# Two more up chunks of each SwiGLU by seven block products, and residues of 105 weight pieces summed by DMAs

## The chip, the cores and the metric

One core of one Trainium2 chip runs the whole program. The metric is the device time of one execution in microseconds. The kernel before takes 2181.22 us, the median of three runs (2180.66 to 2183.26).

## The reference, cut to what matters

A decoder trunk of two layers on 256 tokens of width 2048, in float32. Layer 0 mixes by two groups of attention heads, layer 1 by latent attention; the change leaves both alone. Each layer ends in a SwiGLU feed-forward network (FFN) of inner width 5632:

```python
def swiglu(x, w_gate, w_up, w_down):
    return (jax.nn.silu(x @ w_gate) * (x @ w_up)) @ w_down

for layer in range(DEPTH):            # DEPTH = 2
    ...                               # y = mixer(x)
    x = layer_norm(DEEPNORM_ALPHA * x + y, ln_g[layer, 0], ln_b[layer, 0])
    y = swiglu(x, ffn_w_gate[layer], ffn_w_up[layer], ffn_w_down[layer])
    x = layer_norm(DEEPNORM_ALPHA * x + y, ln_g[layer, 1], ln_b[layer, 1])
```

## The kernel before

**Splitting.** TensorE (PE) multiplies float32 numbers that are rounded (fp32r). To keep accuracy, each operand is split into a rounded part and a residue, and a product is three matmuls: rounded by rounded, rounded by residue, residue by rounded (`mm3`, lines 115 to 118; PE's moving operand is the weight, the stationary one the tokens). `XH` and `XL` hold the two parts of the FFN's input, `YH` and `YL` those of its inner activations.

**Pieces and visits.** Weights come in *chunks* of 512 columns, and a chunk in *pieces* of 256 rows (512 KB). An FFN has gate chunks g0 to g10 and up chunks u0 to u10 of eight pieces each, and down chunks in five groups of four (d0 to d4, after ups 1, 3, 5, 7 and 10). The list `visits` gives the order in which PE uses the pieces; all else follows it. A *plain* visit is 12 matmuls of 512 columns: two blocks of 128 rows, two blocks of tokens, three passes. Chunks marked `S` (gates 1 to 10) are done as seven block products in place of eight, in the manner of Strassen and Winograd: `emit_s` issues 21 matmuls of 256 columns (lines 426 to 428), with sums of blocks of the weights and sums of blocks of the tokens (the tiles `XS`, which `xs_batch` makes in four batches at the start of each FFN). An `S` chunk has four PSUM banks A, B, C, D. When its eighth visit is issued, `drain_s` (lines 456 to 462) adds them up: ACT copies a part of A, then five DVE sums follow, the last two of which read the tile written before; the gate's Silu on ACT comes right behind (line 1023).

**The interleave.** `ffn_part` first lists the plain visits of an FFN in the order u0, u1, d0, u2, u3, d1 and so on (`flat`), and then puts the `S` visits between them: a counter `want` grows by 0.61 per plain visit for 14 visits, then by 0.527, and when it passes a whole number the next gate piece is put in. An up that ends is multiplied on DVE with its gate (`u_done`, line 1027), and `h_T` turns the product by PE transposes after the next plain visits (`after_up`) and splits it into `YH` and `YL`.

**Feeding.** For each piece, in the order of the list, SyncE (SP) issues a load into a raw buffer (`feed_dma`, line 336; four for plain pieces, two, `sraw`, for `S` pieces, and a few more elsewhere). `feed_split` then takes a free pair of weight buffers (in the FFNs four plain pairs `wh`, `wl` and two `S` pairs `sh`, `sl`), and issues for a plain piece the rounding on ACT (line 400) and the residue on DVE (line 402). For an `S` piece `split_s` issues at once the three block differences on DVE (lines 358 to 361, in place in the raw buffer), and *owes* the rounding on ACT (`hi`, line 364) and the residue on DVE (`lo`, line 367, which also frees the raw buffer). Owed work is paid by `pay`:

```python
            while o["fns"] and (step == "all" or o["age"] >= 1 and step == o["fns"][0][0]):
                o["fns"].pop(0)[1]()
```

Each later split raises the age by one. A plain split pays ahead of raising it, so the second plain split after an `S` piece pays; the split of the next `S` piece raises first and then pays, behind its own differences.

**The order of all this** is the program's: the schedule is manual, each engine runs its instructions in the order of issue, and SP its loads. In the main loop a visit is issued, then the chunk's `done` (the drain and the Silu, or the up's product), then the callbacks, and then the buffers of the visited piece become free and `feed_more` issues splits and loads as long as buffers of the right kind are free. An `S` piece's split so comes behind the visit of the `S` piece two before it.

GpSimd (POOL) has little work: parts of the layer norms and of the attention. It issues no DMA.

Of the kernel before, what the change touches and what calls it, by code (L numbers as in the profile page):

```python
# [9 lines left out]
F32 = mybir.dt.float32  # L10
F32R = mybir.dt.float32r
AF = mybir.ActivationFunctionType
ALU = mybir.AluOpType
# [39 lines left out]
def trunk_kernel(ctx: ExitStack, tc: tile.TileContext, x, ab_w_in, b_f, ab_w_out,  # L53
# [81 lines left out]
    def kmajor(c, hs=None):  # L135
        for h in (range(c.nh) if hs is None else hs):
            visits.append((c, h, (0, 1)))
# [57 lines left out]

    GROUPS = ((0, 1), (2, 3), (4, 5), (6, 7), (8, 9, 10))
    NF = 11
    after_up = {}
    win = {}

    def ffn_part(layer):
        def wide(nm, w, f):
            return add_chunk(f"{nm}{layer}_{f}", "X", K16, ([512], lambda h: rows(
                w[layer], h * 256, [(0, 512, f * 512)])))

        def down(gi):
            grp = GROUPS[gi]
            slots = [4 * (f % 4) + k for f in grp for k in range(4)]
            for n in range(4):
                c = add_chunk(f"d{layer}_{gi}_{n}", "Y", slots, (  # L210
                    [512], lambda h, n=n: rows(
                        w_down[layer], grp[0] * 512 + h * 256, [(0, 512, n * 512)])))
                if gi == len(GROUPS) - 1 and n == 3:
                    (lead_final if layer == 1 else lead_end)(c)
                else:
                    kmajor(c)

        g0 = wide("g", w_gate, 0)
        g0.pair = 0
        lead_begin(g0)  # L220
        base = len(visits)
        for f in range(NF):
            kmajor(wide("u", w_up, f))
            if f in (1, 3, 5, 7):
                down(f // 2)
        down(len(GROUPS) - 1)
        flat = visits[base:]
        del visits[base:]
        ends = {}
        for f in range(NF):  # L230
            e = ends[f] = max(k for k, v in enumerate(flat) if v[0].name == f"u{layer}_{f}")
            after_up[layer, f] = [(v[0].name, v[1], v[2]) for v in flat[e + 1:e + 4]]
        gates = []
        for f in range(1, NF):
            c = wide("g", w_gate, f)
            c.S = True
            gates += [(c, h, (0, 1)) for h in range(8)]
        near = {ends[f] + 2 for f in (1, 3, 5, 7, 9)}
        ns, want = 0, 0.0
        for k, v in enumerate(flat):  # L240
            visits.append(v)
            want = max(want + (0.61 if k < 14 else 0.527), ns + 1 if k in near else 0)
            while ns < min(len(gates), int(want)):
                visits.append(gates[ns])
                ns += 1
                if ns % 8 == 0:
                    assert k < ends[ns // 8] - 1, (k, ns, ends)
        assert ns == len(gates)

    w_out_part("oa", ab_w_out[0])  # L250
    ffn_part(0)
# [89 lines left out]
    owed = []  # L341
# [12 lines left out]
    def split_s(j):  # L354
# [14 lines left out]
        wts[j] = (sh.rearrange("p (q c) -> p q c", c=256), sl.rearrange("p (q c) -> p q c", c=256))  # L369
        return hi, lo  # L370

    def feed_split(j, halves=False, part=None):
        if j >= len(pieces):
            return False
        c, h = pieces[j]
        n = 2 * c.n
        if part != 1:
            got = take(w_free, j) if j in raws else None
            if got is None:
                return False  # L380
            slot_of[j] = got
            if c.S:
                new = split_s(j)
                for o in owed:
                    o["age"] += 1
                pay("act")
                pay("dve")
                owe(j, *new)
                return True
            r = raws.pop(j)  # L390
            wh, wl = got[1]
            wts[j] = (wh[:, :n].rearrange("p (k c) -> p k c", k=2),
                      wl[:, :n].rearrange("p (k c) -> p k c", k=2))
            whole[j] = (r, wh, wl)
        r, wh, wl = whole[j]
        cuts = [(0, c.n), (c.n, n)] if halves or part is not None else [(0, n)]
        if part is not None:
            cuts = [cuts[part]]
        for a, b in cuts:
            nc.scalar.activation(wh[:, a:b], r[:, a:b], AF.Copy)  # L400
            pay("act")
            nc.vector.tensor_tensor(wl[:, a:b], r[:, a:b], wh[:, a:b].bitcast(F32),  # L402
                                    op=ALU.subtract)
            pay("dve")
        if part != 0:
            whole.pop(j)
            raw_free.append(rslot_of.pop(j))
        for o in owed:
            o["age"] += 1
        return True  # L410
# [601 lines left out]
    def ffn_done(layer):  # L1012
        for f in range(NF):
            cg, cu = chunks[f"g{layer}_{f}"], chunks[f"u{layer}_{f}"]

            def g_done(t, cg=cg, f=f):
                gt = ff["gt"][f % 2]
                if not cg.S:
                    nc.scalar.activation(gt[:, t], cg.ps[t][0], AF.Silu)
                elif t == 1:  # L1020
                    drain_s(cg, gt)
                    g_ = gt.rearrange("p t c -> p (t c)")
                    nc.scalar.activation(g_, g_, AF.Silu)

            def u_done(t, cu=cu, f=f):
                h_ = ff["gt"][f % 2][:, t]
                nc.vector.tensor_tensor(h_, h_, cu.ps[t][0], op=ALU.mult)

            def h_T(t, f=f):
                h_ = ff["gt"][f % 2][:, t]  # L1030
                tp = transposes([h_[:, k * P:(k + 1) * P] for k in range(4)])
                y = 4 * (f % 4)
                sl = (slice(None), slice(y, y + 4), slice(t * P, (t + 1) * P))
                hilo(YH[sl], YL[sl], tp.rearrange("p (k c) -> p k c", k=4))

            cg.done, cu.done = g_done, u_done
            for t in (0, 1):
                at(after_up[layer, f][t], lambda h_T=h_T, t=t: h_T(t))
        last = len(GROUPS) - 1
        for gi in range(len(GROUPS)):  # L1040
            for n in range(4):
                c = chunks[f"d{layer}_{gi}_{n}"]
                c.done = lambda t, half=None, c=c, n=n, gi=gi: residual(
                    c.ps[t], t, n, gi == 0, gi == last,
                    fine=(layer == 1 and gi == last and t == 1), half=half)
        at((f"g{layer}_0", 3, (1,)), lambda: (xs_open(), xs_batch(0)))
        for n in (1, 2, 3):
            at((f"g{layer}_0", 4 + n, (0, 1)), lambda n=n: xs_batch(n))
        at((f"g{layer}_0", 7, (0, 1)), lambda: s_window(True))
        at(after_up[layer, NF - 1][2], lambda: s_window(False))  # L1050
        at((f"g{layer}_{NF - 1}", 7, (0, 1)), lambda: xs_close(layer))
# [340 lines left out]
```

## Time and profile before

| | |
|---|---|
| median of three runs | 2181.22 us (2180.66 to 2183.26) |
| the profiled execution | 2182.57 us; span on the core 2180.7 us; mean granted clock 0.994 |
| PE busy | 2141.0 us, 98% of the span |
| DVE, ACT, POOL busy | 1645.9 us (75%), 1058.5 us (49%), 93.0 us (4%) |
| DMA | 410 MB, mean 188 GB/s, 56.6% of 16 engines' time |

The span is the time from the first instruction to the last; the profiled execution's own time lies 1.9 us over it. Busy shares are averages over the whole span, so a stage's limit is read from its own stretch. Matmuls are pipelined: what one costs is the distance from its start to the next one's start, not its printed duration. A number in square brackets behind a timeline row is idle time of the engine ahead of that instruction, with what ended it. "PEclk" is the share of full clock that TensorE was granted, 1.00 or 0.50.

### The profile page before, as it was taken

What the parts mean: (1) busy time and instruction counts of PE and PEld (TensorE: products, weight loads), DVE (VectorE), ACT (ScalarE), POOL (GpSimd) and SP (SyncE); (2) the same over time, 40 slices, a digit from 0 to 9 for tenths busy, and PEclk for the clock granted to TensorE, in tenths of its full rate; (3) what the DMA queues carried; (4) which work ended last, traced back from release to release, by engine and by line L of the source; (5) the groups of instructions that cost most, each with busy time, mean ns of one, the idle gap of its engine ahead of it and who ended that gap; (6) DMA issues with size and microseconds to landing.
All of it is one profiled execution on the core that took longest, in us unless ns stands there. A gap on an engine that the chain in (4) does not pass through costs nothing.

```text
span 2180.7 us, 29603 instructions
## 1 busy us (share of the span) xinstructions
PE 2141.0 (98%) x11562; PEld 1827.3 (84%) x11562; DVE 1645.9 (75%) x2103; ACT 1058.5 (49%) x1240; POOL 93.0 (4%) x142
## 2 busy tenths in 40 slices
PE   9999999989999999999999999999999999999998
PEld 8788888778888888888878898878888888888886
DVE  5555656798878888888756676698888888788875
ACT  4444544354444454444534676344545444444451
POOL 2100000100000000000001331010000000000000
PEclk9999999999999999999999999999999999999999
DMA  8565555445556555565765544725655556555572
GB/s 286 169 201 165 169 178 205 181 164 188 189 193 203 193 193 193 183 202 190 253 196 163 175 130 132 279 97 181 197 197 189 192 193 203 193 177 184 190 277 80
DMA packets 230332, 410.29 MB, mean 188 GB/s; under 512 B 14088, under 2 KB 58160, under 8 KB 229168
## 3 DMA queue, kind: packets, MB, share of 16 engines
q1 hardware_dynamic: 230192, 408.40, 56.6%
q8 instruction: 91, 1.49, 0.3%
q14 instruction: 49, 0.40, 0.1%
HBM read 402.56 MB, written 5.78 MB: 187 GB/s over the span
## 4 chain that ended last, share of the span: by engine, by line
PE 60%; issue 35%; DVE 4%; POOL 1%; ACT 1%; DMA 0%; SPq 0%; DVEq 0%; POOLq 0%; ACTq 0%
PE mm L116 15%; PE mm L117 15%; PE mm L118 15%; PE tp L545 2%; PE att L117 1%; PE att L118 1%; PE att L116 1%; PE sB L427 1%; PE sB L426 1%; PE sA L427 1%; PE sB L428 1%; PE sC L426 1%; PE sC L427 1%; PE sC L428 1%; PE sA L428 1%
## 5 line engine op out<-in xcount | busy, mean ns | idle before, releaser
L400 ACT ACTIVATE wh<-raw 128x1024 fp32r<-128x1024 f32 (+4 forms) x440 | 457.9, 1045 | 573.6 <-PE mm L118 430.3
L402 DVE TENSOR_TENSOR wl<-raw,wh 128x1024 fp32r<-128x1024 f32 (+4 forms) x440 | 531.5, 1212 | 203.2 <-ACT wh L400 194.9
L116 PE MATMUL mm<-wh,XH 128*128 128x512 f32 (+3 forms) x1120 | 442.0, 395 | 0.5 <-ACT wh L400 0.5
L117 PE MATMUL mm<-wl,XH 128*128 128x512 f32 (+3 forms) x1120 | 436.1, 389 | 1.8 <-DVE wl L402 1.8
L118 PE MATMUL mm<-wh,XL 128*128 128x512 f32 (+3 forms) x1120 | 434.9, 388 | 1.5 <-DVE XL L113 1.5
L367 DVE TENSOR_TENSOR sl<-sraw,sh 128x1792 fp32r<-128x1792 f32 x160 | 323.7, 2023 | 41.8 <-ACT sh L364 41.7
L116 PE MATMUL mm<-wh,YH 128*128 128x512 f32 (+1 forms) x768 | 304.2, 396 | 0.1
L117 PE MATMUL mm<-wl,YH 128*128 128x512 f32 (+1 forms) x768 | 303.2, 395 | 0.0
L118 PE MATMUL mm<-wh,YL 128*128 128x512 f32 (+1 forms) x768 | 303.1, 395 | 0.0
L364 ACT ACTIVATE sh<-sraw 128x1792 fp32r<-128x1792 f32 x160 | 270.4, 1690 | 13.2 <-DVE sraw L361 13.2
L118 PEld LDWEIGHTS mm<-wh,XL 128*128 128x128 f32 x1120 | 210.6, 188 | 49.2 <-DVE XL L113 2.4
L116 PEld LDWEIGHTS mm<-wh,XH 128*128 128x128 f32 x1120 | 211.5, 189 | 41.4 <-ACT wh L400 1.0
L117 PEld LDWEIGHTS mm<-wl,XH 128*128 128x128 f32 x1120 | 211.0, 188 | 41.5 <-DVE wl L402 2.6
L118 PEld LDWEIGHTS mm<-wh,YL 128*128 128x128 f32 x768 | 144.2, 188 | 35.0
L116 PEld LDWEIGHTS mm<-wh,YH 128*128 128x128 f32 x768 | 144.6, 188 | 31.1 <-ACT qk L764 0.3
L117 PEld LDWEIGHTS mm<-wl,YH 128*128 128x128 f32 x768 | 144.2, 188 | 31.2
L358 DVE TENSOR_TENSOR sraw<-sraw 128x512 f32<-128x512 f32 x160 | 109.5, 684 | 19.4 <-DMA sraw<-in_ffn_w_gate_dram 19.4
L427 PE MATMUL sA<-sl,XH 128*128 128x256 f32 x320 | 90.3, 282 | 7.7 <-DVE sl L367 7.7
L426 PE MATMUL sA<-sh,XH 128*128 128x256 f32 x320 | 92.9, 290 | 3.4 <-ACT sh L364 3.4
L427 PE MATMUL sB<-sl,XS 128*128 128x256 f32 x320 | 90.7, 284 | 0.0
L426 PE MATMUL sB<-sh,XS 128*128 128x256 f32 x320 | 90.7, 283 | 0.0
L428 PE MATMUL sB<-sh,XS 128*128 128x256 f32 x320 | 90.7, 283 | 0.0
(266 smaller groups left out, 3572.9 us busy)
## 6 DMA issues: line engine op xcount, KB each, us to landing
raw<-in_ffn_w_up_dram SPq DMA_DIRECT2D x174, 512.0 KB, 4.8
sraw<-in_ffn_w_gate_dram SPq DMA_DIRECT2D x164, 512.0 KB, 3.7
raw<-in_ffn_w_down_dram SPq DMA_DIRECT2D x160, 512.0 KB, 5.7
raw<-in_ab_w_in_dram SPq DMA_DIRECT2D x80, 256.0 KB, 3.2
sraw<-in_ab_w_in_dram SPq DMA_DIRECT2D x48, 256.0 KB, 3.1
raw<-in_ab_w_out_dram SPq DMA_DIRECT2D x22, 512.0 KB, 3.7
raw<-in_mla_w_out_dram SPq DMA_DIRECT2D x21, 512.0 KB, 3.7
raw<-in_ab_w_in_dram SPq DMA_DIRECT2D x18, 512.0 KB, 3.7
```

Source lines behind the costliest of these rows:

```text
L116: nc.tensor.matmul(o, lh, rh, start=start, stop=False)
L117: nc.tensor.matmul(o, lh, rl, start=False, stop=False)
L118: nc.tensor.matmul(o, ll, rh, start=False, stop=stop)
L358: nc.vector.tensor_tensor(v[:, 4:6], v[:, 0:1].broadcast_to([P, 2, 256]), v[:, 1:3], op=ALU.subtract)
L364: nc.scalar.activation(sh, r[:, 256:2048], AF.Copy)
L367: nc.vector.tensor_tensor(sl, r[:, 256:2048], sh.bitcast(F32), op=ALU.subtract)
L400: nc.scalar.activation(wh[:, a:b], r[:, a:b], AF.Copy)
L402: nc.vector.tensor_tensor(wl[:, a:b], r[:, a:b], wh[:, a:b].bitcast(F32), op=ALU.subtract)
L426: nc.tensor.matmul(o, h, w[0][:, q], start=first, stop=False)
L427: nc.tensor.matmul(o, h, w[1][:, q], start=False, stop=False)
L428: nc.tensor.matmul(o, l, w[0][:, q], start=False, stop=last)
L545: nc.tensor.transpose(tp[:, i * P:(i + 1) * P], s_, ident)
```

## The change

Up chunks 4 and 8 of each FFN become `S` chunks: they leave the list of plain visits, and their pieces stand behind those of gates 4 and 8 in the list of `S` visits (gates 1 to 4, up 4, gates 5 to 8, up 8, gates 9 and 10). The counter grows by 0.725 per plain visit throughout. When such an up ends, `drain_s` writes it into the tile `xt`, and one DVE product of 1024 columns follows; its transposes come behind the next two visits.

For 105 plain pieces (`by_dma`: pieces 5 to 7 of gate 0, all of up 0, and every third plain up or down piece between an FFN's first and last `S` piece) the residue isn't made on DVE. ACT rounds the piece, copies the rounded part with its sign turned into `wl`, and GpSimd issues a DMA that adds the raw piece to it. Such a split raises the age of owed work first and then pays.

```diff
--- before.py
+++ after.py
@@ -195,6 +195,8 @@
 
     GROUPS = ((0, 1), (2, 3), (4, 5), (6, 7), (8, 9, 10))
     NF = 11
+    UPS = (4, 8)
+    h_done = set()
     after_up = {}
     win = {}
 
@@ -220,7 +222,11 @@
         lead_begin(g0)
         base = len(visits)
         for f in range(NF):
-            kmajor(wide("u", w_up, f))
+            c = wide("u", w_up, f)
+            if f in UPS:
+                c.S = True
+            else:
+                kmajor(c)
             if f in (1, 3, 5, 7):
                 down(f // 2)
         down(len(GROUPS) - 1)
@@ -228,24 +234,32 @@
         del visits[base:]
         ends = {}
         for f in range(NF):
-            e = ends[f] = max(k for k, v in enumerate(flat) if v[0].name == f"u{layer}_{f}")
-            after_up[layer, f] = [(v[0].name, v[1], v[2]) for v in flat[e + 1:e + 4]]
+            if f not in UPS:
+                e = ends[f] = max(k for k, v in enumerate(flat) if v[0].name == f"u{layer}_{f}")
+                after_up[layer, f] = [(v[0].name, v[1], v[2]) for v in flat[e + 1:e + 4]]
         gates = []
         for f in range(1, NF):
             c = wide("g", w_gate, f)
             c.S = True
             gates += [(c, h, (0, 1)) for h in range(8)]
+            if f in UPS:
+                gates += [(chunks[f"u{layer}_{f}"], h, (0, 1)) for h in range(8)]
         near = {ends[f] + 2 for f in (1, 3, 5, 7, 9)}
         ns, want = 0, 0.0
         for k, v in enumerate(flat):
             visits.append(v)
-            want = max(want + (0.61 if k < 14 else 0.527), ns + 1 if k in near else 0)
+            want = max(want + 0.725, ns + 1 if k in near else 0)
             while ns < min(len(gates), int(want)):
                 visits.append(gates[ns])
                 ns += 1
-                if ns % 8 == 0:
-                    assert k < ends[ns // 8] - 1, (k, ns, ends)
+                c = gates[ns - 1][0]
+                f = int(c.name[3:])
+                if ns % 8 == 0 and c.name[0] == "g" and f not in UPS:
+                    assert k < ends[f] - 1, (k, ns, ends)
         assert ns == len(gates)
+        for f in UPS:
+            e = max(k for k, v in enumerate(visits) if v[0].name == f"u{layer}_{f}")
+            after_up[layer, f] = [(v[0].name, v[1], v[2]) for v in visits[e + 1:e + 3]]
 
     w_out_part("oa", ab_w_out[0])
     ffn_part(0)
@@ -368,6 +382,21 @@
             raw_free.append(rslot_of.pop(j))
         wts[j] = (sh.rearrange("p (q c) -> p q c", c=256), sl.rearrange("p (q c) -> p q c", c=256))
         return hi, lo
+
+    nth = {}
+    for j, (c, h) in enumerate(pieces):
+        if not c.S:
+            nth[j] = len(nth)
+
+    def by_dma(j):
+
+        c, h = pieces[j]
+        if c.name in ("g0_0", "g1_0"):
+            return h >= 5
+        if c.name in ("u0_0", "u1_0"):
+            return True
+        y = c.name[1]
+        return c.name[0] in "ud" and y in first_s and first_s[y] < j < last_s[y] and nth[j] % 3 == 0
 
     def feed_split(j, halves=False, part=None):
         if j >= len(pieces):
@@ -393,6 +422,17 @@
                       wl[:, :n].rearrange("p (k c) -> p k c", k=2))
             whole[j] = (r, wh, wl)
         r, wh, wl = whole[j]
+        if part is None and by_dma(j):
+            nc.scalar.activation(wh[:, :n], r[:, :n], AF.Copy)
+            nc.scalar.activation(wl[:, :n], wh[:, :n].bitcast(F32), AF.Copy, scale=-1.0)
+            nc.gpsimd.dma_start(out=wl[:, :n].bitcast(F32), in_=r[:, :n], accum_op=ALU.add)
+            whole.pop(j)
+            raw_free.append(rslot_of.pop(j))
+            for o in owed:
+                o["age"] += 1
+            pay("act")
+            pay("dve")
+            return True
         cuts = [(0, c.n), (c.n, n)] if halves or part is not None else [(0, n)]
         if part is not None:
             cuts = [cuts[part]]
@@ -1018,15 +1058,23 @@
                 if not cg.S:
                     nc.scalar.activation(gt[:, t], cg.ps[t][0], AF.Silu)
                 elif t == 1:
+                    assert f < 2 or (layer, f - 2) in h_done
                     drain_s(cg, gt)
                     g_ = gt.rearrange("p t c -> p (t c)")
                     nc.scalar.activation(g_, g_, AF.Silu)
 
             def u_done(t, cu=cu, f=f):
                 h_ = ff["gt"][f % 2][:, t]
-                nc.vector.tensor_tensor(h_, h_, cu.ps[t][0], op=ALU.mult)
+                if not cu.S:
+                    nc.vector.tensor_tensor(h_, h_, cu.ps[t][0], op=ALU.mult)
+                elif t == 1:
+                    drain_s(cu, ff["xt"].rearrange("p (t c) -> p t c", t=2))
+                    g_ = ff["gt"][f % 2].rearrange("p t c -> p (t c)")
+                    nc.vector.tensor_tensor(g_, g_, ff["xt"], op=ALU.mult)
 
             def h_T(t, f=f):
+                if t == 1:
+                    h_done.add((layer, f))
                 h_ = ff["gt"][f % 2][:, t]
                 tp = transposes([h_[:, k * P:(k + 1) * P] for k in range(4)])
                 y = 4 * (f % 4)
```

## Rows read from the trace of the kernel before

**Rows 1.** The page, parts 1 and 5 (columns as in rows 5).
```profile
PE 2141.0 (98%) x11562; PEld 1827.3 (84%) x11562; DVE 1645.9 (75%) x2103; ACT 1058.5 (49%) x1240; POOL 93.0 (4%) x142
...
L400 ACT ACTIVATE wh<-raw 128x1024 fp32r<-128x1024 f32 (+4 forms) x440 | 457.9, 1045 | 573.6 <-PE mm L118 430.3
```

**Rows 2.** Busy time of each engine by stretch, middle of FFN 0.
```profile
core 0: us, PE busy (x) PEld busy (x) DVE busy (x) ACT busy (x) POOL busy (x), PEclk, DMA share, GB/s
510.00:1060.00 550.00, 548.32 (x3114) 475.37 (x3113) 461.65 (x524) 270.01 (x236) 0.00 (x0) 1.00 0.58 193
```

**Rows 3.** Busy time by stretch, same columns, the two FFN starts.
```profile
425.00:475.00 50.00, 41.52 (x199) 33.41 (x198) 46.24 (x60) 27.16 (x27) 0.26 (x1) 0.93 0.43 148
...
1430.00:1485.00 55.00, 47.51 (x224) 38.30 (x222) 51.55 (x66) 28.00 (x31) 4.36 (x3) 0.94 0.39 131
```

**Rows 4.** Timeline of PE in FFN 0: start us, us, instruction.
```profile
502.24 0.28 PE L426 MATMUL sA<-sh,XH 128*128 128x256 f32 x1
...
504.71 0.39 PE L116 MATMUL mm<-wh,XH 128*128 128x512 f32 x1
...
507.50 0.40 PE L116 MATMUL mm<-wh,XH 128*128 128x512 f32 x1
```

**Rows 5.** Groups by line, DVE, 510 to 1060: count, busy us, mean ns.
```profile
L402 DVE TENSOR_TENSOR wl<-raw,wh 128x1024 fp32r<-128x1024 f32 x132 | 160.8, 1223 | 51.5 <-ACT wh L400 47.6
```

**Rows 6.** Timeline, FFN 0, one seven-product piece prepared beside the next.
```profile
477.01 0.37 SPq L336 DMA_DIRECT2D sraw<-in_ffn_w_gate_dram  x1
...
478.58 1.71 ACT L364 ACTIVATE sh<-sraw 128x1792 fp32r<-128x1792 f32 x1
...
480.64 0.69 DVE L358 TENSOR_TENSOR sraw<-sraw 128x512 f32<-128x512 f32 x1 [0.78 <-DMA sraw<-in_ffn_w_gate_dram]
...
482.17 2.02 DVE L367 TENSOR_TENSOR sl<-sraw,sh 128x1792 fp32r<-128x1792 f32 x1
...
484.21 0.37 SPq L336 DMA_DIRECT2D sraw<-in_ffn_w_gate_dram  x1
```

**Rows 7.** DMA issues, 510 to 1060: count, KB, us to landing.
```profile
raw<-in_ffn_w_up_dram SPq DMA_DIRECT2D x71, 512.0 KB, 5.3
...
sraw<-in_ffn_w_gate_dram SPq DMA_DIRECT2D x70, 512.0 KB, 3.7
```

**Rows 8.** Timeline of POOL and DVE before FFN 0's start.
```profile
421.82 1.75 POOL L946 TENSOR_TENSOR X<-X,G 128x512 f32<-128x512 f32 x1 [2.97 <-ACT X L945]
...
422.46 1.66 DVE L929 SCALAR_TENSOR_TENSOR X<-X,mv,B 128x512 f32<-128x512 f32 x1
...
425.85 0.75 DVE L929 SCALAR_TENSOR_TENSOR X<-X,mv,B 128x512 f32<-128x512 f32 x1
```

**Rows 9.** Timeline around the end of gate 1 in FFN 0.
```profile
510.33 0.28 PE L426 MATMUL sA<-sh,XH 128*128 128x256 f32 x1
...
511.23 0.39 ACT L456 ACTIVATE gt<-sA 128x256 f32<-128x256 f32 x1 [0.83 <-PE sA L428]
...
512.37 0.41 DVE L457 TENSOR_TENSOR gt<-gt,sD 128x256 f32<-128x256 f32 x1
...
515.12 1.06 ACT L1023 ACTIVATE gt<-gt 128x1024 f32<-128x1024 f32 x1 [3.50 <-DVE gt L462]
```

**Rows 10.** Timeline of four PE waits in the FFNs.
```profile
461.49 0.39 PE L426 MATMUL sA<-sh,XH 128*128 128x256 f32 x1 [1.62 <-ACT sh L364]
...
464.35 0.58 PE L427 MATMUL sA<-sl,XH 128*128 128x256 f32 x1 [2.47 <-DVE sl L367]
...
892.64 0.66 PE L545 MATMUL tp<-ident,gt 128*128 128x128 f32 x4 [1.55 <-DVE gt L1027]
...
1905.31 0.66 PE L545 MATMUL tp<-ident,gt 128*128 128x128 f32 x4 [2.15 <-DVE gt L1027]
```

**Rows 11.** Busy time by stretch, same columns, around the last of these waits.
```profile
1907.00:1910.00 3.00, 3.00 (x15) 2.90 (x15) 2.39 (x3) 2.13 (x2) 0.00 (x0) 0.50 0.00 0
...
1902.00:1912.00 10.00, 7.85 (x40) 6.83 (x40) 9.04 (x12) 5.13 (x5) 0.00 (x0) 0.83 0.37 140
```

## The prediction

> **What bounds the kernel now.** I read the page's engine line first: PE is busy 2141.0 of 2180.7 us [rows 1], so only PE work that goes, or PE waits that come or go, move the time. Then busy time by stretch for the changed code: between 510 and 1060 us, the middle of FFN 0, PE is busy 548.32 of 550 us at full clock while DVE has 461.65 us (84%) and ACT 270.01 (49%) [rows 2]. There PE is the limit and nothing waits. Only the two FFN starts are different: in 425 to 475 PE has 41.52 of 50 us, in 1430 to 1485 47.51 of 55, with DVE at 46.24 and 51.55, and the granted clock averages 0.93 and 0.94 [rows 3]. So DVE bounds the starts, PE the rest.
>
> In the order of time, a seven-product visit runs from 502.24 to 504.71 (2.47 us) and a plain one from 504.71 to 507.50 (2.79 us) [rows 4].
>
> I write s for the start of a chunk's last seven-product visit, "next chunk" for the seven-product chunk after it, "hi" for the ACT rounding at L364 and "lo" for the DVE residue at L367.
>
> **Part 1: 32 plain visits become seven-product visits** (2 chunks x 8 pieces x 2 layers): 32 x (2.79 - 2.47) = **-10.2 us**. This is PE time in a stretch where PE is the limit, so it counts in full.
>
> **Part 2: the residues done by DMAs.** 53 pieces in FFN 0 and 52 in FFN 1 each lose a 1.22 us DVE instruction [rows 5] and gain an ACT copy like L400's, 1.05 us [rows 1], and a GpSimd DMA. DVE per layer: 16 pieces go from 1.22 us to 3.55 (1.53 us from 480.64 to 482.17 for the differences, 2.02 for lo [rows 6]), +37 us; 53 x 1.22 = 65 us go. ACT gets 53 x 1.05 + 16 x (1.71 - 1.05) = 66 us on 49% busy. Neither becomes the bound by its sum.
> - At the FFN starts 11 residues a layer (gate 0's last three, up 0's eight) leave a DVE that is nearly full: 11 x 1.22 = 13.4 us. What PE loses there is 8.48 + 7.49 us idle, and 7% of 50 and 6% of 55 us by the clock, 3.5 + 3.3: 22.8 us in all [rows 3]. The gain is at most all of it. It is not, since DVE still has the four XS batches and two S pieces there, and up 0's pieces 2 and 3 are rounded on ACT only behind hi of gate 1's first pieces, two copies and a DMA before use. Their DMA may end late by some us, at worst 2 us per piece for two pieces in two layers beyond what is saved (+4). I take half: **-11.4 us** (ends -22.8 and +4).
> - In the middle a DMA's sum has time: its piece is rounded about three seven-product and three plain visits before PE needs it, 3 x 2.47 + 3 x 2.79 = 15.8 us; less a hi of 1.71 and two copies of 1.05 some 12 us are left. No accumulating DMA is in the trace. The nearest rows are the plain loads of the same 512 KB, 3.7 us (gates) and 5.3 us (ups, several queued) from issue to landing [rows 7]; one that reads two streams could be twice the larger, 10.6. All lie under 12, so **0**; above 12 it is rival 2. The raw buffer stays taken longer, and SP, which issues loads in order, waits there: that load is wanted four plain pieces later (over 16 us), and the S load behind it waits on a lo that comes later still.
> - GpSimd beside DVE: a DVE instruction that takes 0.75 us alone took 1.66 beside a GpSimd tensor operation [rows 8]. If each of 105 DMAs did that, DVE would lose 0.9 us each, under 50 us a layer, which about eats what it is relieved of; I count 0.
>
> By the Trainium skill (SBUF — State Buffer, "Who interferes with whom") a DVE instruction with two SBUF inputs contends with a GpSimd instruction that reads SBUF, not with one that only writes. The measured pair agrees [rows 8]; that a DMA's issue is free of it no run here shows. By the skill (DMA: Bandwidth & Descriptors, "Anatomy of one DMA — SWDGE (gpsimd) path") a GpSimd DMA takes about 2.0 us plus its bytes at 436 GB/s, an estimate of 3.2 us for 512 KB; by that figure the starts would give back nearly all and the sum below would be 11 us lower.
>
> **Part 3: the new interleave, and what it does at chunk ends.** This is the costly part. With 0.725 seven-product visits a plain visit there are now one or two plain visits between two of them, and at all 22 places where a chunk ends and the next begins there is just one (before: two, but for one place a layer).
>
> How a seven-product piece is prepared: its hi and lo are owed, and paid by the second plain split after it, by the first one that goes by DMA, or else by the next S piece's split, behind its differences. That last case is in [rows 6]: hi ran at 478.58, but lo waited on DVE behind the next piece's differences, which waited for the load issued at 477.01; lo came at 482.17. Where just one plain piece that is not summed by DMA follows a piece, this holds. If that piece is the first of a chunk, the split that pays for it comes after the visit that ends the old chunk, whose drain and Silu are put on the queues ahead of it. By the code's order this is so at 12 of the 22 places (after gates 1, 2, 4, 6, 9 and ups 4, 8 in FFN 0; after gates 2, 3, 5, 9 and up 4 in FFN 1); before it was so at none.
>
> Its time, from the drain of gate 1 [rows 9]: s is 510.33, the copy ends at s + 1.29, the DVE sums run from 512.37 until Silu starts at 515.12, 2.75 us (there behind a lo; with DVE free they start right after the copy): s + 4.1. Silu 1.06: s + 5.2. Then hi 1.71 and lo 2.02 [rows 6]: s + 8.9. PE would want that lo at s + 2.47 + 2.79 + 0.12 = s + 5.4. It waits 1.5 us for hi and 2 us for lo, 3.5 in all. After an up (3 of the 12) there is no Silu, but a 1.2 us product and the next differences (1.53) before lo: again s + 8.9, less 0.35 us that PE spends on transposes: 3.1 us. Sum 9 x 3.5 + 3 x 3.1 = **+40.8 us** (36 to 46, some 0.4 us less or more at each).
>
> Such waits lower the clock too. Waits of 1.62 and 2.47 us around one matmul at 461 to 464 [rows 10] lie in the stretch whose clock averages 0.93 [rows 3], and one of 2.15 us was followed by half clock (0.50 at 1907 to 1910; 0.83 over 1902 to 1912, which is 1.7 us lost [rows 11]); after the 1.55 us at 892 matmuls kept their full pace [rows 10]. Mine are 3.5 us with one matmul between; I let 10 of 12 lose 1.7 us: **+17 us** (0 to 35, the upper at the 2.9 us or so of the worst start).
>
> Elsewhere hi and lo are early enough: at the other 10 chunk ends the second piece of the chunk is ready about when PE comes. In the middle the loop of [rows 6], load, differences, lo, load, takes 484.21 - 477.01 = 7.2 us a piece against 5.26 of PE with one plain visit, so such a piece eats 1.9 us of lead; with two plain visits (8.05) 0.9 comes back. Two such in a row nearly always follow a double, which costs 1.1 of some 3 us of lead: 0 (up to 15 if loads take 5.3 us, as ups do).
>
> **Part 4: waits that go.** Twice a gate's drain held up the product of an up that ended beside it, and PE's transposes waited 1.55 and 2.15 us, the second with 1.7 us of clock [rows 10]. No up ends there now: **-5.4 us** (-5.4 to 0).
>
> **Sum:** -10.2 - 11.4 + 40.8 + 17 - 5.4 = +30.8 us, on the profiled execution's 2182.57 us (span 2180.7 and 1.9 around it) 2213.4. That execution was 1.35 us above the median of the three, so the forecast is **2212 us** as a median, slower by 1.4%.
>
> **Rivals.**
> 1. *The chunk ends don't hold PE* (the other side). What speaks for it: at all 18 such places before, PE did not wait. Then -10.2, up to -22.8 and -5.4: 2143 to 2154 us. Against it: both queues kept the program's order in [rows 6, 9]. It decides if lo of a chunk's first piece ends by s + 5.4. Chance 0.07.
> 2. *The DMAs' sums are late or in DVE's way.* If they take more than 12 us, each of some 83 in the middle holds PE; at 1.5 us each +125 us on the forecast: about 2337. For it: nothing in the trace shows such a DMA, and GpSimd slowed DVE in [rows 8]. Against: loads of that size take 3.7 to 5.3 us. Chance 0.08.
> 3. *It cancels.* Waits at chunk ends as computed but hardly any clock loss, and the starts fully relieved: -10.2 - 22.8 - 5.4 + 40.8 = +2.4 to about -4: 2177 to 2186. Chance 0.12.
> The forecast has 0.73.
>
> **Numbers.** The terms' own ends give 2180 (starts fully relieved, no clock loss) to 2266 (all at their worst at once, which I cut to 2250); rivals 1 and 2 lie outside. Range 2180 to 2250. Within 0.2% means 2176.9 to 2185.6 us, about what a measurement of this kernel can tell. Faster: rival 1 and a part of 3, 0.11; same: most of 3 and the forecast's lower end, 0.11; slower 0.78.
>
> **What the changed profile would show.** Part 1: 3360 + 672 matmuls at the mm_s lines, 2.47 us a visit. Part 3: PE waits "<-ACT sh" of about 1.5 us and "<-DVE sl" of about 2 us, some twelve times, each right after a drain's Silu, and the clock under 1.00 behind them. Part 2: L402 down by 105 and 32, POOL's DMAs landing within 12 us, PE idle at the starts under 8 us. Waits on "wl" that a DMA ends, in the middle, would be rival 2. No PE wait at the chunk ends would make the prediction wrong.

## The result and the profile after

The changed kernel takes 2356.38 us (median of 4 runs, 2346.64 to 2361.95) against 2182.24 of the kernel before beside it: ratio 1.0796, interval 1.078 to 1.0812. The forecast was slower by 1.4%; it is slower by 8%, and 2356 lies outside 2180 to 2250. The profiled execution took 2355.63 us, span 2353.8, mean granted clock 0.975 (before 0.994).

The page, engines and DMA queues (columns as in [rows 1]; a queue's packets, MB, share of 16 engines' time):

```profile
PE 2195.6 (93%) x11850; PEld 1871.9 (80%) x11850; DVE 1602.8 (68%) x2110; ACT 1188.0 (50%) x1349; POOL 184.2 (8%) x247
...
q1 hardware_dynamic: 230192, 408.40, 52.7%
q0 software_dynamic: 15120, 55.06, 12.3%
```

PE was the limit and now stands idle 158 us of the span, and no other engine is near its own: DVE fell from 75% to 68%. So no engine is the bound; PE stands because pieces are late. (q1 holds SP's loads, q0 GpSimd's sums: 55.06 MB are 105 of them.) Busy time by stretch answers to [rows 2, 3]: the middle of FFN 0 loses 50 of 550 us, and neither start has gained (the second now lies at 1527 to 1582).

```profile
425.00:475.00 50.00, 40.78 (x201) 32.66 (x200) 35.50 (x50) 35.43 (x35) 9.25 (x11) 0.97 0.88 220
510.00:1060.00 550.00, 499.78 (x2813) 432.30 (x2812) 392.76 (x464) 279.30 (x242) 29.50 (x34) 0.96 0.68 198
...
1527.00:1582.00 55.00, 47.71 (x236) 38.63 (x235) 38.11 (x52) 40.09 (x39) 10.47 (x12) 0.94 0.89 220
```

PE's waits over the whole span (us, times, longest), the largest groups; the list sums to 146.6 us in 109 waits, before to 29.0 in 28:

```profile
PE sA L467 <- DVE sl L381: 58.9, 40, 3.3
PE mm L117 <- DMA wl<-raw: 32.7, 28, 4.6
PE tp L585 <- DVE gt L1069: 16.8, 8, 4.4
PE sA L466 <- ACT sh L378: 15.4, 15, 1.4
PE mm L116 <- DVE YL L113: 6.8, 2, 6.5
PE sA L466 <- DVE gt L498: 3.6, 2, 2.2
```

The end of gate 1 (answers to [rows 9]), ACT, DVE and PE:

```profile
510.16 0.28 PE L466 MATMUL sA<-sh,XH 128*128 128x256 f32 x1
...
514.24 1.06 ACT L1064 ACTIVATE gt<-gt 128x1024 f32<-128x1024 f32 x1 [2.79 <-DVE gt L502]
...
515.21 1.68 ACT L378 ACTIVATE sh<-sraw 128x1792 fp32r<-128x1792 f32 x1
...
516.92 2.02 DVE L381 TENSOR_TENSOR sl<-sraw,sh 128x1792 fp32r<-128x1792 f32 x1 [1.19 <-ACT sh L378]
...
516.94 0.39 PE L466 MATMUL sA<-sh,XH 128*128 128x256 f32 x1 [1.35 <-ACT sh L378]
...
519.00 0.47 PE L467 MATMUL sA<-sl,XH 128*128 128x256 f32 x1 [1.67 <-DVE sl L381]
```

This is the wait of Part 3 as forecast: Silu at s + 4.1, lo's end at s + 8.8 (8.9 foretold). The clock of the 15 us around it is 0.89, 1.65 us lost:

```profile
510.00:525.00 15.00, 11.97 (x65) 10.49 (x64) 10.41 (x14) 7.57 (x7) 0.86 (x1) 0.89 0.51 155
```

DMA issues from 510 to 1060 (answers to [rows 7]: count, KB, us to landing). All loads land later than before: 3.7 became 4.6 for the gates, 5.3 became 6.1 for the plain ups.

```profile
raw<-in_ffn_w_down_dram SPq DMA_DIRECT2D x61, 512.0 KB, 6.6
sraw<-in_ffn_w_gate_dram SPq DMA_DIRECT2D x58, 512.0 KB, 4.6
raw<-in_ffn_w_up_dram SPq DMA_DIRECT2D x40, 512.0 KB, 6.1
wl<-raw POOLq DMA_DIRECT2D x34, 512.0 KB, 8.3
```

**The 173 us of span, added up.** Listed waits +117.6. A listed wait leaves out some 0.26 us (at 519.00 the row says 1.67, but the step from 516.94 is 2.06 in place of 0.12, 1.94 lost): 81 more waits, +21. Clock: 2353.8 x 0.025 less 2180.7 x 0.006, +45.8. PE's work -10.2. Together +174. Of the 117.6, the 12 chunk ends make 35.2, other waits on a seven-product piece's hi and lo +28.0 (39.1 against 11.1), two waits on a drain that still read the PSUM bank +3.6, waits on a DMA's sum (less those on the residues that it replaces) +30.9, transposes +13.1, YH and YL +9.5, the rest -2.7.

### The profile page after: what moved, and what is told of

Read it like the earlier page. It is cut to its first block, busy times and chain, and to the rows that moved or that the text cites. A ratio compares the mean times of both kernels' runs of the same rounds, so it can differ in the third digit from the quotient of the medians.

```text
span 2353.8 us, 30582 instructions
## 1 busy us (share of the span) xinstructions
PE 2195.6 (93%) x11850; PEld 1871.9 (80%) x11850; DVE 1602.8 (68%) x2110; ACT 1188.0 (50%) x1349; POOL 184.2 (8%) x247
## 3 DMA queue, kind: packets, MB, share of 16 engines
q1 hardware_dynamic: 230192, 408.40, 52.7%
q0 software_dynamic: 15120, 55.06, 12.3%
## 5 line engine op out<-in xcount | busy, mean ns | idle before, releaser
L440 ACT ACTIVATE wh<-raw 128x1024 fp32r<-128x1024 f32 (+4 forms) x303 | 315.0, 1041 | 489.2 <-DMA raw<-in_ffn_w_down_dram 196.1
L381 DVE TENSOR_TENSOR sl<-sraw,sh 128x1792 fp32r<-128x1792 f32 x192 | 387.9, 2022 | 166.3 <-ACT sh L378 166.3
L442 DVE TENSOR_TENSOR wl<-raw,wh 128x1024 fp32r<-128x1024 f32 (+4 forms) x303 | 364.8, 1205 | 191.2 <-ACT wh L440 189.9
L117 PE MATMUL mm<-wl,XH 128*128 128x512 f32 (+3 forms) x988 | 389.9, 395 | 27.7 <-DMA wl<-raw 27.4
L116 PE MATMUL mm<-wh,XH 128*128 128x512 f32 (+3 forms) x988 | 391.6, 396 | 0.0
L118 PE MATMUL mm<-wh,XL 128*128 128x512 f32 (+3 forms) x988 | 385.4, 390 | 0.6 <-DVE XL L113 0.6
L378 ACT ACTIVATE sh<-sraw 128x1792 fp32r<-128x1792 f32 x192 | 324.4, 1690 | 60.0 <-DVE sraw L375 54.4
L428 POOL DMA_DIRECT2D wl<-raw x104 | 90.3, 868 | 1343.5 <-ACT wl L427 1209.6
L426 ACT ACTIVATE wh<-raw 128x1024 fp32r<-128x1024 f32 x104 | 109.7, 1055 | 99.3 <-DMA raw<-in_ffn_w_up_dram 57.5
L467 PEld LDWEIGHTS sA<-sl,XH 128*128 128x128 f32 x384 | 75.7, 197 | 75.8 <-DVE sl L381 70.3
```

The lines of the kernel that those rows point to most:

```text
L116: nc.tensor.matmul(o, lh, rh, start=start, stop=False)
L117: nc.tensor.matmul(o, lh, rl, start=False, stop=False)
L118: nc.tensor.matmul(o, ll, rh, start=False, stop=stop)
L378: nc.scalar.activation(sh, r[:, 256:2048], AF.Copy)
L381: nc.vector.tensor_tensor(sl, r[:, 256:2048], sh.bitcast(F32), op=ALU.subtract)
L426: nc.scalar.activation(wh[:, :n], r[:, :n], AF.Copy)
```

## The experiments

**1. Which half costs?** First theory, called H in the expectations: a raw buffer held by a sum makes SP late. First rival: the interleave does it all.

```diff
-        if part is None and by_dma(j):
+        if False and by_dma(j):
```

> The change with every residue on DVE again (no sum by DMA), ups 4 and 8 and the new interleave kept. Theory H (held buffers): a sum keeps its raw buffer until it lands some 8 us after its issue, SP issues loads in order and stands behind that buffer, so all loads come late, and with them the roundings and residues of all pieces. Then only the 12 chunk ends hold PE here: 2182.6 - 10.2 + 38.4 (9 x 3.29 + 3 x 2.92 as the changed kernel shows) + 17 of clock - 5.4 = 2222 us, 2205 to 2235, and no PE wait on a residue at other pieces. Rival I (interleave): the denser seven-product pieces alone outrun the feeding (7.2 us a piece against 6.3 of PE), and the sums are bystanders: then 2300 us or more, with some 25 waits on residues at second to eighth pieces of chunks.

2278.29 us, ratio 1.0437 (1.0385 to 1.049). Neither number: the interleave costs 95 us without a single sum, twice what I gave it. The forecast's 12 places became 18 (53.2 us of listed waits), because a sum's split pays owed work at once and so had spared six; and the clock is 0.976, 54.7 us of the span against 13.1.

```profile
PE sA L467 <- DVE sl L381: 54.6, 32, 3.7
PE sA L466 <- ACT sh L378: 22.4, 16, 1.7
```

```diff
-    UPS = (4, 8)
+    UPS = ()
-            want = max(want + 0.725, ns + 1 if k in near else 0)
+            want = max(want + (0.61 if k < 14 else 0.527), ns + 1 if k in near else 0)
```

> The sums by DMA with the interleave of before and all ups plain. Theory H: loads are late here too; PE has more time per seven-product piece (7.8 us against 6.3), so less shows than in the changed kernel: 2220 to 2320 us, with PE waits on residues that a late load starts. Rival I: the sums cost nothing and relieve the starts: 2160 to 2185 us.

2202.54 us, 1.0079 (1.0051 to 1.0108): under H's range and over the rival's. With 2.47 + 2.79 / 0.527 = 7.8 us of PE per seven-product piece the sums alone cost 19 us. They do relieve the starts of waits on hi and lo (no such wait is left in the whole kernel), and put their own in their place:

```profile
PE mm L117 <- DMA wl<-raw: 16.0, 12, 2.9
PE tp L585 <- DVE gt L1069: 14.0, 12, 2.4
```

The sums' bytes by themselves hardly make the loads late: in the middle of FFN 0 the DMA engines are busier here than in the change (0.80 against 0.68) with more sums (43 against 34), and by the median the loads land about as before (3.9 and 5.3 us against 3.7 and 5.3):

```profile
510.00:1060.00 550.00, 543.22 (x3069) 470.22 (x3068) 401.37 (x473) 310.74 (x276) 37.38 (x43) 1.00 0.80 232
```

```profile
sraw<-in_ffn_w_gate_dram SPq DMA_DIRECT2D x69, 512.0 KB, 3.9
raw<-in_ffn_w_up_dram SPq DMA_DIRECT2D x68, 512.0 KB, 5.3
...
wl<-raw POOLq DMA_DIRECT2D x43, 512.0 KB, 5.2
```

```diff
+        return False
         y = c.name[1]
         return c.name[0] in "ud" and y in first_s ...
```

> The change with sums by DMA only for gate 0's end and up 0 (11 pieces a layer), none in the middle. Theory H: the middle as in the kernel without sums, and since PE stands idle as long at the first start as before (40.8 of 50 us busy in the changed kernel), the starts give little: within 8 us of the kernel without sums, 2205 to 2230. Rival I: over 2290 us.

2283.13 us, 1.0459 (1.0429 to 1.049): as without sums, and out of the range with it. Within the spread of the runs the 22 sums at the starts neither cost nor gain; the 78 us between 2278 and 2356 belong to the sums in the middle. They are a net figure, since the sums' splits also spare six chunk ends.

**2. The orders of paying.**

```diff
+                    pay("all")
                     drain_s(cg, gt)
```

> No sums by DMA, and at the end of each seven-product chunk the owed rounding and residue of the next chunk's first piece are put on the queues ahead of the drain. If the chunk ends cost what the order of the queues says, their 38 us and the clock lost behind them go: 10.2 + 5.4 under before, less the drain being late by up to 3.7 us, which PE doesn't wait for: 2168 us, 2160 to 2180. Rival: the wait only moves, to the Silu and the sums of the drain that free the PSUM banks of the next chunk or to the transposes of the next up: 2200 us or more, with PE waiting on the drain's tiles.

2229.15 us, 1.0212 (1.016 to 1.0265), over the range: the rival's time, but PE's waits aren't on the drain. Behind no chunk end does PE wait any more, and 49 us go: the chunk ends are shown, and so is that they are half of the 95. What is left is the loop of [rows 6], here in this kernel:

```profile
523.61 2.02 DVE L381 TENSOR_TENSOR sl<-sraw,sh 128x1792 fp32r<-128x1792 f32 x1
524.41 1.69 ACT L378 ACTIVATE sh<-sraw 128x1792 fp32r<-128x1792 f32 x1
525.65 0.37 SPq L350 DMA_DIRECT2D sraw<-in_ffn_w_gate_dram  x1
529.85 0.69 DVE L372 TENSOR_TENSOR sraw<-sraw 128x512 f32<-128x512 f32 x1 [1.90 <-DMA sraw<-in_ffn_w_gate_dram]
...
531.38 2.02 DVE L381 TENSOR_TENSOR sl<-sraw,sh 128x1792 fp32r<-128x1792 f32 x1
533.42 0.37 SPq L350 DMA_DIRECT2D sraw<-in_ffn_w_gate_dram  x1
```

A residue frees the buffer, SP loads (4.2 us), the differences wait for that load, and the residue of the piece whose hi ended at 526.1 stands behind them: 7.77 us from load to load. PE needs 2.47 + 1.38 x 2.79 = 6.3 us a piece (96 pieces beside some 132 plain visits).

```diff
+                for o in owed:
+                    o["age"] += 1
+                pay("act")
+                pay("dve")
                 new = split_s(j)
-                for o in owed: ...   (the same lines, moved up)
```

> No sums by DMA, a chunk's first piece paid ahead of the drain (2229 us), and now also: at the split of a seven-product piece the owed rounding and residue of the piece before are put on the queues ahead of its block differences, not behind them. Theory L (the loop residue, load, differences, next residue of 7.8 us a piece starves PE in the middle of chunks): the some 20 waits at second to sixth pieces outside the FFN starts and their clock go, 28 us and 13 us: 2188 us, 2175 to 2200. Rival: the differences come late instead, the waits move to the rounding of the next piece: 2215 us or more.

2195.56 us, 1.0061 (1.0038 to 1.0084), 34 us less, and DVE's differences, which waited 68.1 us for gate loads, wait 0.3: the loop is shown. Both orders of paying together are 83 of the 95 us.

```profile
PE sA L467 <- DVE sl L381: 12.5, 14, 1.7
...
DVE sraw L372 <- DMA sraw<-in_ffn_w_gate_dram: 0.3, 1, 0.3
```

**3. What in a sum costs?**

```diff
-            nc.scalar.activation(wl[:, :n], wh[:, :n].bitcast(F32), AF.Copy, scale=-1.0)
-            nc.gpsimd.dma_start(out=wl[:, :n].bitcast(F32), in_=r[:, :n], accum_op=ALU.add)
+            nc.scalar.activation(wl[:, :n], r[:, :n], AF.Copy)
+            nc.gpsimd.dma_start(out=wl[:, :n].bitcast(F32), in_=wh[:, :n].bitcast(F32), accum_op=ALU.add)
```

> The changed kernel, but ACT copies the raw piece into wl and the DMA adds the rounded part to it, in place of the reverse: same copies, same bytes moved, but the raw buffer is free when ACT has read it, not when the DMA has landed (the residue of these 105 pieces is then raw plus rounded part, not the difference). Theory H (held raw buffers make SP issue the loads late): most of what the sums cost goes. Without sums, 19 chunk ends waited; with the sums' earlier paying 12 do, so 2278 less some 7 x 5 = 2245 us, 2225 to 2275, and raw loads land at their old 5.3 us or are at least issued earlier. Rival C (the sums' traffic or ACT's copies slow everything): it stays at 2330 us or above.

2360.79 us, 1.082 (1.0782 to 1.0858): as slow as the change, though SP waits for no sum any more between 510 and 1060. H falls. SP's waits there in the changed kernel would have said so: it stands for lo, hardly for a sum.

```profile
SPq L350 <- DVE sl L381: 418.4, 71, 10.9
SPq L350 <- DMA wl<-raw: 16.4, 4, 4.7
```

```diff
-            nc.gpsimd.dma_start(out=wl[:, :n].bitcast(F32), in_=r[:, :n], accum_op=ALU.add)
+            nc.gpsimd.dma_start(out=wl[:, :64].bitcast(F32), in_=r[:, :64], accum_op=ALU.add)
```

> The changed kernel, but each DMA sum adds only the first 64 of 1024 columns (the other columns keep the negative rounded part as residue): the copies on ACT, the issues on GpSimd and the way of paying stay, the bytes and most of the time to landing go. Theory H: the buffer is held for a shorter time, so about as without the hold, 2225 to 2290 us. Rival C, if traffic is the cost: the same; if ACT's two copies or GpSimd's issue are the cost: 2330 us or above. Together with the run that frees the raw buffer early this tells hold, traffic and copies apart.

2248.56 us, 1.0306 (1.0272 to 1.034): 108 us go with the bytes (and with them 960 of 1024 columns of the residue), and the copies and issues that stay are not the cost. It even lies 30 us under the kernel without sums: only the forecast's 12 chunk ends wait here, not 18. So what else comes with a sum gains a little, and its bytes cost more than the net 78. The loads are quick again:

```profile
sraw<-in_ffn_w_gate_dram SPq DMA_DIRECT2D x64, 512.0 KB, 4.1
raw<-in_ffn_w_down_dram SPq DMA_DIRECT2D x64, 512.0 KB, 5.4
raw<-in_ffn_w_up_dram SPq DMA_DIRECT2D x46, 512.0 KB, 4.9
...
wl<-raw POOLq DMA_DIRECT2D x37, 32.0 KB, 4.6
```

Bytes could act through the loads or through the sum's own late landing. The next run puts bytes back without a sum that needs them (to the small sum's two lines of above):

```diff
+            nc.gpsimd.dma_start(out=scr[0][:, :n], in_=wh[:, :n].bitcast(F32))
+            nc.gpsimd.dma_start(out=scr[1][:, :768], in_=wh[:, :768].bitcast(F32))
```

> The kernel whose sums add only 64 columns (2248.6 us), and beside each such sum GpSimd issues two plain copies of the rounded part to memory outside the core, 512 and 384 KB (together 1.75 times a load's bytes: a full sum took 44.5 us of DMA engine time in the changed kernel, 12.3% of 16 engines' 2353.8 us over 104, a 512 KB load about 25). Nothing on the path waits for these copies. Theory T (the sums' bytes slow all other loads, and these set the feeding loops): about as slow as the changed kernel, 2320 us or more, with loads landing in 4.6 us and 6 us or more. Theory W (it is the late landing of the sum itself that PE waits for and that keeps pairs of buffers): 2245 to 2270 us, and loads a little slower without effect.

2352.14 us, 1.0782 (1.0739 to 1.0825): the whole 104 us are back, and the loads are as late as in the change. One flaw: 34 times GpSimd waited for a copy to land before it issued the next (63 us in all), so some small sums were late too, and PE's waits on them are 25.4 us against 32.7 in the change and 5.4 without the copies. So the run shows that the bytes cost, and doesn't part late loads from late sums.

```profile
raw<-in_ffn_w_down_dram SPq DMA_DIRECT2D x59, 512.0 KB, 6.3
sraw<-in_ffn_w_gate_dram SPq DMA_DIRECT2D x57, 512.0 KB, 4.8
raw<-in_ffn_w_up_dram SPq DMA_DIRECT2D x42, 512.0 KB, 6.5
...
PE sA L470 <- DVE sl L382: 66.2, 44, 3.7
PE mm L118 <- DMA wl<-raw: 25.4, 13, 5.2
```

The waits say more on the way. From 64 columns to the whole sum PE's listed waits grow by 68 us: on hi and lo of seven-product pieces by 33 (41.5 to 74.3), on the sums by 27 (5.4 to 32.7), the transposes and others by the rest. DVE's block differences wait twice as long for their load. First row 64 columns, second the change, third the run that comes next:

```profile
DVE sraw L372 <- DMA sraw<-in_ffn_w_gate_dram: 35.4, 30, 3.2
```

```profile
DVE sraw L372 <- DMA sraw<-in_ffn_w_gate_dram: 71.0, 44, 4.0
```

```profile
DVE sraw L372 <- DMA sraw<-in_ffn_w_gate_dram: 0.5, 1, 0.5
```

With both orders mended and all sums kept (the edits of the two runs of part 2):

> The changed kernel with all its sums by DMA, but with both orders mended: a chunk's first piece paid ahead of the drain, and the owed residue ahead of the next differences. Theory H: the sums still hold raw buffers, loads still come late, so it stays well above the same kernel without sums: 2230 to 2300 us. Rival: the sums were only bad because the loop was tight, and with the loop mended they cost little: 2200 us or less.

2275.19 us, 1.0428 (1.0398 to 1.0458), 80 us above the same kernel without sums. The range held, but its reason (held buffers) had fallen. The 80 us are near the 78 of before, but not for the same reason: with the order mended the differences no longer wait for their load (last row above), so the loop carries nothing here. PE's listed waits grow by 52 us over the kernel without sums: on the sums 19.9, on lo 13.6, on transposes 14.8 and smaller ones. And the pair differs in more than bytes: a sum's split, at a third of the plain pieces, pays owed work early, which by itself, at all of them, costs 60 us in the kernel without sums (first run of part 4). How much of the 80 us is the bytes' no run shows.

**4. Can the 10 us be had?** Paying one plain split earlier:

```diff
+        if part is None and c.name[0] in "ud" and c.name[2:3] == "_":
+            for o in owed:
+                o["age"] += 1
         cuts = ...
```

> No sums by DMA, first piece of a chunk paid ahead of the drain, residue ahead of the next differences (2195.6 us), and now also a plain FFN piece's split pays what is owed at once, not the second one. If what is left in the middle (some 6 us of waits on residues and the clock behind them) is late paying: 2188 us, 2178 to 2192. Rival: what is left has another cause (waits for YH by the down pieces and at the starts): 2193 to 2200 us.

2255.34 us, 1.0338 (1.0318 to 1.0359): a miss, 60 us worse. The waits that were to go are still there: behind the FFN starts six of 8 us, at second pieces. And the rounding now comes to the head of ACT before its differences are done, and ACT's other work stands behind it (first two rows ACT, without and with; last row PE with, 8.2 us without):

```profile
ACT sh L378 <- DVE sraw L375: 193.9, 102, 4.7
```

```profile
ACT sh L378 <- DVE sraw L375: 310.1, 134, 4.8
...
PE tp L588 <- DVE gt L1073: 27.2, 11, 5.0
```

The same edit with one up, and with none (the kernel before with early paying and the residue ahead of the differences):

```diff
-    UPS = (4, 8)
+    UPS = (8,)
-            want = max(want + 0.725, ...
+            want = max(want + (0.59 if k < 108 else 0.7), ...
```

> As the kernel with early paying, but only up 8 by seven block products, with a counter of 0.59 per plain visit up to the 108th and 0.7 behind it: 16 plain visits fewer in place of 32, 5.1 us of PE work saved on the kernel before. With two plain visits between many pieces the middle has the slack of the kernel before: 2178 us, 2172 to 2186. Rival: the stretch of 0.7 behaves as the whole change does and gives the 5 us back: 2183 to 2195.

2208.63 us, 1.0125 (1.0105 to 1.0145): a miss, over both ranges.

> The kernel before with only the two mended orders of paying (at the first plain split; residue ahead of the next differences). PE waits there only at the FFN starts and for some transposes, so hardly anything can be won: 2177 to 2184 us. Rival: paying earlier relieves the FFN starts, where hi and lo of gate 1's first pieces are late: down to 2165 us.

2193.12 us, 1.0054 (1.0036 to 1.0072): over the range; even the kernel before loses 12 us, and by the last run of this part, which has the other edit alone, it is the early paying that loses them. Without early paying, the same one up:

> Only up 8 by seven block products (5.1 us of PE work saved), no sums by DMA, counter 0.59 up to the 108th plain visit and 0.7 behind it, first piece paid ahead of the drain, residue ahead of the next differences, and owed work again paid by the second plain split. If early paying cost the 60 us that the two kernels with both ups differ by, because the rounding waits at the head of ACT for its differences, this one gains in proportion to its dense stretch: 2208 down to 2185 us, 2178 to 2192. Rival: the loss of 2208 came from the dense stretch at the end: 2200 us or more.

2184.09 us, 1.0013 (1.0003 to 1.0024): in the range, the best with any up by seven products, and not better than before.

> The same single up and counter with the orders of paying of before. It tells whether two plain visits between most pieces are enough by themselves: some 3 or 4 of the 11 chunk ends a layer then have one plain visit, 3.3 us and 1.7 us of clock each, about 8 x 5 = 40 us less the 5 us: 2210 us, 2195 to 2230. Rival: the loop of residue, load and differences only fails with both ups: 2180 to 2190 us.

2198.09 us, 1.008 (1.006 to 1.01): at the lower end of the range, but not as reckoned. Six chunk starts wait, by half a microsecond each, not 8 by 3.3; with two plain visits at most places the orders of paying cost 14 us in place of 83.

> The kernel before with only one edit: at the split of a seven-product piece the owed residue goes ahead of the next differences. In the middle of its FFNs PE waits for no residue, so there is nothing to win: 2179 to 2184 us. Rival: with the residue ahead its raw buffer is free sooner and the loads come earlier, which helps the FFN starts: down to 2172 us.

2181.6 us, 1.0 (0.999 to 1.001): as expected, no difference. No version here beats the kernel before.

## Why the prediction was wrong, step by step

The forecast missed by 144 us. By the runs some 53 of them are the interleave (95 us in place of 42), some 73 the sums in the middle (0 forecast), and 16 the starts (-11.4 forecast, +5 in the run with sums there alone, within its spread).

- **Part 1.** 192 groups of 21 matmuls are in the trace, at the length that was read (2.48 us from 637.93 to 640.41). The -10.2 us are small beside the rest; no run shows them alone.
- **Part 2, the middle: the step that failed.** "All lie under 12, so 0" priced a sum by its own landing. That guess held: 4.5 to 11.3 us, median 7.7. What I left out is what its bytes do to the other 512 KB loads: q0 took 12.3% of 16 engines' 2353.8 us over 105 sums, 44.1 us of engine time each, where a load takes 25.5 (q1's 52.7% over 408.40 MB). The runs with 64 columns and with the copies show that these bytes cost 104 to 108 us in the order of the change. There the seven-product loads land 0.5 us later (4.6 against 4.1 with 64 columns), and I had the loop that turns this into time before me in [rows 6], at 7.2 us a piece: DVE's differences wait 71.0 us for gate loads in place of 35.4 with 64 columns. It isn't the only way, since the waits on the sums themselves grow nearly as much as those on hi and lo. What each way is worth was not measured, nor why the same bytes leave the loads alone in the loose interleave.
- **Part 2, the lead of a sum.** "Some 12 us are left" was wrong too: in the middle of the FFNs PE waited 17 times for a sum, 14.2 us in all. In the rows below the rounding itself waited for a late load, and PE wanted the residue at 640.81 (642.28 less 1.47), 10.4 us behind the rounding's start in place of 15.8; the sum, issued at 632.98, took 9.3.

```profile
630.42 1.06 ACT L426 ACTIVATE wh<-raw 128x1024 fp32r<-128x1024 f32 x1 [2.23 <-DMA raw<-in_ffn_w_up_dram]
...
632.98 0.86 POOL L428 DMA_DIRECT2D wl<-raw  x1 [14.87 <-ACT wl L427]
...
642.28 0.50 PE L117 MATMUL mm<-wl,XH 128*128 128x512 f32 x1 [1.47 <-DMA wl<-raw]
```

- **Part 2, the starts.** -11.4 was forecast; there is no gain (40.8 of 50 us busy, before 41.5; 47.7 of 55, before 47.5). DVE was relieved (46.2 to 35.5 us), but PE waits 12.3 us for the sums between 420 and 500, with the DMA engines 85% busy.
- **Part 2, GpSimd beside DVE.** Right at 0: the residues take 2022 and 1221 ns, before 2024 and 1223.
- **Part 3, chunk ends.** The 12 places are the 12 that were named, nine with 1.51 + 1.94 us from step to step and three with 2.92: 39.8 us; 40.8 were forecast. The clock at these places was near the forecast as well: in the 15 us around each, PEclk was 0.89 at eight, 0.77 at two, 0.81 and 1.00 at one, 23 us lost where 17 were forecast. The other half of the +46 us of clock lies elsewhere, where the forecast had no waits.
- **Part 3, "elsewhere hi and lo are early enough".** Wrong: I let the 7.2 us loop eat lead only now and then ("0, up to 15"). It is 34 us without sums, by the run that put the residue ahead of the differences.
- **Part 4.** -5.4 became +13: transposes wait longer for the product of gate and up (L1069). Why each of the eight does, no run took apart.
- **The rivals.** Rival 2's time, 2337, was near, in good part by luck: no sum took more than 12 us and DVE was not slowed, and of its 83 waits of 1.5 us in the middle 17 came, 14.2 us in all. Its sign, waits on wl in the middle, did show. Its chance of 0.08 was too low, since "nothing in the trace shows such a DMA" is a reason for wide bounds, not for a low chance. Rival 1 fell with the 12 waits; rival 3 needed no clock loss and relieved starts, and got neither.
- **The range.** With every term at its worst the sum is some 2271, not 2266; 2356 lies over either.

By the Trainium skill (DMA: Bandwidth & Descriptors, "Anatomy of one DMA — SWDGE (gpsimd) path") the estimate was 3.2 us for 512 KB; the trace differs, 7.7 us beside other loads, and 4.4 us even for the 32 KB of the run with 64 columns.

Open: what part of the sums' cost comes by late loads and what by late sums; what the bytes cost once the order is mended; and the 14 us by which the mended kernel with both ups (2195.56) stays above the kernel before, though it saves 10. Its waits for YL (8.5 us in two) and transposes name a place; no run changed them. The interleave with raw buffers to spare wasn't tried.

## What to carry to other kernels

Before work is moved from a compute engine to DMAs, ask what their bytes do to the loads already there, in the schedule that they will meet: here such sums cost 19 us in the loose interleave and a net 78 in the dense one. Find the loop that a load closes (free buffer, load, first use, free buffer) and compare its length with what the bound engine needs per piece; where the loop is the longer of the two, a later load can become time once per piece. When a denser schedule uses up the slack, the order in which owed work is queued decides: two edits of order were worth 83 us in the dense schedule, and the one of them that the kernel before could take was worth nothing there. Paying earlier is not always better, it lost 60 us in the same dense schedule. Read what the issuing queue waits for before building a theory on held buffers, and look for what else differs between two runs before a difference is given to one cause.

## What the runs showed of the hardware

In the change an accumulating DMA of 512 KB within the core took 44.1 us of DMA engine time, 1.7 times the 25.5 of a load of the same bytes, and landed in 7.7 us (5.9 in the loose interleave); one of 32 KB still took 4.4. Issuing 105 of them from GpSimd left DVE's residues at their old length (2022 and 1221 ns, before 2024 and 1223), where a GpSimd tensor operation had doubled one [rows 8].
